# Eighty expert keys and sixty gathers ahead, a third place for weight parts between attention and the queries, and a first-block gather rate of 258/305, in a hybrid layer on Trainium2

## The chip, the cores and the metric

The kernel runs on one core of a Trainium2 chip. The metric is the device time of one execution in microseconds (us), as the median of several runs. The engines of a core run side by side, each through its own instruction list in order: TensorE (PE, with its weight loads PEld), VectorE (DVE), ScalarE (ACT), GpSimd (POOL) and SyncE (SP). They wait for each other by semaphores. DMA queues that the engines issue move the data between memory and the on-chip buffer.

## The reference, cut to what matters

One layer on x of 512 tokens by 2048, all in float32:

```python
h = hybrid_mixer(x, ...)             # mLSTM branch + forgetting attention, gated, @ w_out
x = layer_norm(DN_ALPHA * x + h, ...)
h = memory_cross_attention(x, mem, w_q, w_kv, w_o)     # 256 memory rows, 4 heads
x = layer_norm(DN_ALPHA * x + h, ...)
h = peer_ffn(x, peer_wq, sub_keys, expert_u, expert_v)
x = layer_norm(DN_ALPHA * x + h, ...)
```

The mixer's attention has 16 heads of 128 with a decay; its output Y goes through w_branch_fox and a gate. The experts (peer_ffn) are what most of the change is about. Each token has 8 heads; each picks its 16 best of 128 x 128 = 16384 experts by two lists of 128 sub-keys. With idx and g the 128 picks of a token and their weights:

```python
a = einsum('tkd,td->tk', expert_u[idx], xt)
h = gelu(a) * g
out = einsum('tk,tkd->td', h, expert_v[idx])
```

## The kernel before, in words

**Two token blocks.** Block A is the first 128 tokens, block B the other 384. A goes through the mixer, both norms, the cross attention and its expert picks early, woven into B's mixer, so that its experts' rows can be gathered while B's products run.

**Weights.** A weight comes as a raw tile of 512 KB (128 x 1024) on SP's queue (`load_raw`, L141). ScalarE rounds it to a high part `whi` (`split`, L133), VectorE subtracts to get the low part `wlo` (L134), and a product is three matmuls: high by high, high by low, low by high (`products`, L196 to L201). Other operands are split in the same way (`Ah`, `Al` by `load_split`, L136 to L139). The places for raw tiles and parts come from a list of rings, used in turn: W has 3 raw places and 2 each for `whi` and `wlo`; until the end of attention the list is W, w1 (2 raw, 1 and 1), W, and after `xs.close()` it is W alone (L1152), until the experts, when W and a ring E of the gate pool alternate.

**Pacing by weights.** `load_w` (L177 to L190) also drives gathers: for each weight loaded it adds `work["rate"]` to an account and issues as many gather steps as the account holds. The steps wait by an added dependency for the `wlo` of that weight. `residual` (L715 to L735) holds the gathers in its last two groups until the norm is done.

**Small steps.** `mid` puts small steps on a list, and `ride` takes one off for each weight loaded; a `None` is an empty turn, and `settle` runs what is left. Attention (`fox`, L580 ff) uses this. It works in quads of four heads through a written list of steps (L692): k, q, v products, S (scores, L678), g (gates of the branch), T (transposes of the probabilities and the results, L682). T(3) stands ahead of g(3), the last group. The results go to memory (`hold_r`, L1145), to `ytd`. `merge` (L700 ff) then reads `ytd` back as rows `Ah`, `Al`, five ahead (`Rows`, `load_split`), and multiplies with `w_br_fx`.

**The order.** A scheduler in the framework orders each engine's instructions by priority and simulated readiness when the kernel is compiled. On the chip each engine runs its list in that order, and a late operand holds all that is behind it.

**The experts.** A's 128 tokens are gathered in full: `gathered(0, 0, P, ...)` (L911 ff) has 258 steps: 128 rows of u (a product with the token on VectorE, L934), 128 of v (multiplied and added, L937), each row set fetched by an indirect DMA from POOL (L906), three row buffers, and a closing norm (L981 to L992) with two stores on SP's queue. It starts in the mixer of B with a rate of 258/290 steps a weight. Of B's tokens, 104 are gathered in the same way (211 steps), and 280 are taken densely: for each of the 128 keys c, `stage_a(c)` (L1279 ff) multiplies all 280 tokens with the 128 experts of that key (48 matmuls of 280 columns into `sm`), takes the gelu on ScalarE (`ga`, L1291), and for c under LOOK stores it to memory (`gad`). `stage_h` (L1297 ff) multiplies with the gates (L1308), read from `gd`, and splits the result to `hph`, `hpl`; `stage_o` takes a chunk of J = 8 keys times the v rows (`po`) and adds to `acc` (L1436).

**The gates.** The picks (`select`, with `soften`, L803 to L857, on VectorE) for B's gathered tokens come inside the query stage, those for the dense tokens after it. Then the gates are built in 70 blocks of four tokens: two comparisons on VectorE (L1253), four scalings on ScalarE (L1258), four products of 128 x 128 on PE (L1259, two records each), four copies on ScalarE (L1262), and, for each 32 tokens, stores to `gd` from ScalarE's queue (L1264). LOOK = 72 keys are done ahead of the expert chunks, and the scheduler weaves the last of them with the gates; EARLY = 56 of the 211 gather steps ride along with these keys, the rest with the chunks.

Of the kernel before, what the change touches and what calls it, by code (L numbers as in the profile page):

```python
# [10 lines left out]
F32 = mybir.dt.float32  # L11
# [10 lines left out]
P = 128  # L22
# [23 lines left out]
def build(tc, I, out):  # L46
    nc = tc.nc
    with ExitStack() as ctx:
        cp = ctx.enter_context(tc.tile_pool(name="const", bufs=1))
        dp = ctx.enter_context(tc.tile_pool(name="scratch", bufs=1, space=DRAM))  # L50
        def weights(stack, name, raw, hi, lo):

            return dict(pool=stack.enter_context(tc.tile_pool(name=name, bufs=1, reuse_waits="tile")), raw=raw, hi=hi, lo=lo)


        W = weights(ctx, "w", 3, 2, 2)
        rings = [W]
# [16 lines left out]
        def nm(s):  # L74
            cnt[0] += 1
            return f"{s}_{cnt[0]}"
# [64 lines left out]
        def load_raw(src, n=1024):  # L141
            rings.append(rings.pop(0))
            ring = rings[-1]
            raw = ring["pool"].tile([P, n], F32, tag="raw", bufs=ring["raw"], name=nm("raw"))
            nc.sync.dma_start(raw, src)
            return raw


        work = {"jobs": None, "rate": 0.0, "due": 0.0, "last": None, "hold": False,
                "quiet": 0, "normed": None}  # L150
# [12 lines left out]
        def mid(*steps):  # L163
            mids.extend(steps)
# [100 lines left out]
        for kt in range(8):  # L265
            raw = load_raw(I["xT"][kt])
# [313 lines left out]
        def fox(R, fp, ft, hold):  # L580
            n, b0, nb = R.n, R.b0, R.nb
# [71 lines left out]
            def turn_p(qd, s, kbs):  # L653
                Q = quads[qd]
                for kb in kbs:
                    f = max(kb, b0)
                    bank = sm_bank()
                    for qb in range(f, b0 + nb):
                        nc.tensor.transpose(bank[:, (qb - f) * P:(qb - f + 1) * P],
                                            Q["p"][s][qb - b0][:, kb * P:(kb + 1) * P], ident)  # L660
                    m = (b0 + nb - f) * P
                    t = fp.tile([P, m], F32, tag=f"pt{kb}", bufs=2, name=nm("fpt"))
                    if kb % 2:
                        nc.scalar.copy(t, bank[:, :m])
                    else:
                        nc.vector.tensor_copy(t, bank[:, :m])
                    Q["t"].setdefault(s, []).append(t)
# [13 lines left out]

            def T(qd):  # L682
                half = (b0 + nb + 1) // 2
                for s in range(4):
                    mid(lambda s=s: turn_p(qd, s, range(half)))
                    if s:
                        mid(lambda s=s: (result(qd, s - 1), turn_p(qd, s, range(half, b0 + nb))))
                    else:
                        mid(lambda s=s: turn_p(qd, s, range(half, b0 + nb)))
                mid(lambda: result(qd, 3))  # L690

            k, q, v, g = keys, queries, values, gates  # L692
            for step in ((k, 0), (q, 0), (v, 0), (S, 0), (g, 0), (T, 0), (k, 1), (q, 1), (v, 1), (S, 1), (g, 1),
                         (T, 1), (k, 2), (q, 2), (v, 2), (S, 2), (k, 3), (T, 2), (q, 3), (v, 3), (S, 3), (g, 2),
                         (T, 3), (g, 3)):
                work = step[0](step[1])
# [201 lines left out]
        def after(i, other):  # L898

            if other is not None:  # L900
                tc.add_manual_dep(i.ins, other.ins.name, mybir.DependencyInfo(
                    mybir.DependencyClass.Sync, mybir.DependencyReason.DATA), reason="pace")
# [8 lines left out]
        def gathered(t, r0, n, i, last, lag, keep=None):  # L911


            ei, gg = eid[:, ecols[i]], egg[:, ecols[i]]
            xacc = gat.tile([P, D], F32, tag="xacc", bufs=1, name=nm("xacc"))
            for j in range(0, P, n):
                nc.gpsimd.dma_start(xacc[j:j + n], x2d[t, r0:r0 + n].rearrange("p g c -> p (g c)"))
            dots = gat.tile([P, P], F32, tag="dots", bufs=2, name=nm("dots"))
            held = []

            def use():
                s, rows = held.pop(0)
                k = s % n
                if s == n:

                    al = gat.tile([P, 1], F32, tag="al", bufs=1, name=nm("al"))
                    if n < P:
                        nc.vector.memset(al, 0.0)
                    nc.vector.memset(al[:n], ALPHA)
                    nc.scalar.mul(xacc, xacc, al)  # L930
                    nc.scalar.activation(dots[:, :n], dots[:, :n], AF.Gelu)
                    nc.vector.tensor_mul(dots[:, :n], dots[:, :n], gg[:, :n])
                if s < n:
                    after(nc.vector.scalar_tensor_tensor(rows, rows, 1.0, xacc, op0=ALU.mult, op1=ALU.mult,  # L934
                                                         accum_out=dots[:, k:k + 1]), last())
                else:
                    after(nc.vector.scalar_tensor_tensor(xacc, rows, dots[:, k:k + 1], xacc,  # L937
                                                         op0=ALU.mult, op1=ALU.add), last())

            for s in range(2 * n):  # L940
                if len(held) == lag:
                    use()
                held.append((s, gather_rows("peer_v" if s >= n else "peer_u", ei, s % n, last)))
                yield True
            while held:
                use()
            if n < P:
                fold = gat.tile([P, 64], F32, tag="fold", bufs=1, name=nm("fold"))
                nc.vector.tensor_add(fold[:, :n], ident[:, 0:n], ident[:, n:2 * n])
                for j in range(2 * n, P, n):  # L950
                    nc.vector.tensor_add(fold[:, :n], fold[:, :n], ident[:, j:j + n])
                for g in range(4):
                    bank = BK["pool"].tile([P, 512], F32, tag="s1", bufs=1, name=nm("fo"))
                    o = xacc[:, g * 512:(g + 1) * 512]
                    nc.tensor.matmul(bank[:n], fold[:, :n], o, start=True, stop=True)  # L955
                    nc.scalar.copy(o[:n], bank[:n])  # L956
            if keep is not None:
                nc.gpsimd.dma_start(keep, xacc[:n])
                yield True
                return  # L960
            lw = fin_load(gat)
            fin_stats(i, xacc, range(4), n)
            fin(t * P + r0, i, xacc, lw, n)
            yield True
# [29 lines left out]
        def run(gen):  # L994
            for _ in gen:
                pass
# [115 lines left out]
            weave(chain(merge(A, YA, GA, ac, at), tail_a()), heads, 0.36)  # L1112

        gat = ctx.enter_context(tc.tile_pool(name="gat", bufs=1, side="right", reuse_waits="tile"))
        work.update(jobs=gathered(0, 0, P, 0, lambda: work["last"], 2), rate=258 / 290)
        run(heads)
        sgp = ctx.enter_context(ExitStack())
        sg = sgp.enter_context(tc.tile_pool(name="sg", bufs=1, side="right", reuse_waits="tile"))
# [30 lines left out]
            run(fox(B, fp, lambda n: fp.tile([P, n], F32, tag="c", bufs=16, name=nm("c")), hold_r))  # L1149
            settle()  # L1150
        xs.close()
        rings[:] = [W]  # L1152
        x3 = ctx.enter_context(ExitStack())
        apool = x3.enter_context(tc.tile_pool(name="acts_a", bufs=1, reuse_waits="tile"))
        cs = ctx.enter_context(ExitStack())
        b2 = cs.enter_context(tc.tile_pool(name="acts_c", bufs=1, side="right", reuse_waits="tile"))

# [3 lines left out]
        with tc.tile_pool(name="xb", bufs=1, reuse_waits="tile") as xp:  # L1161
# [23 lines left out]
            run(residual(B, xp, lambda t, g: x1d[t, :, g], O, zd, lambda i: a_tile(), tmp, r, sts, 4))  # L1185
            norm(B, r, sts[1], 1, x2d, cpair, tmp, X2, x2td)
        x3.close()


        NC_ = PKEYS  # L1190
# [47 lines left out]
        for hb in range(NDENSE // GB):  # L1238
            while turned * P < (hb + 1) * GB:
                bank = o_bank()  # L1240
                n = min(P, NDENSE - turned * P)
# [28 lines left out]
        acc = mn.tile([P, NK, NDENSE], F32, tag="acc", name="acc")  # L1270

        J = 8
        LOOK = 72
        EARLY = 56
        fetched, hs, gates = {}, {}, {}

        rings[:] = [W, E]
# [1 line left out]
        def stage_a(c):  # L1279
# [11 lines left out]
            nc.scalar.activation(ga, bank, AF.Gelu)  # L1291
            if c < LOOK:
                nc.scalar.dma_start(gad[c], ga)
# [3 lines left out]
        def stage_h(c):  # L1297

            for f in range(c, min(c + 3, NC_)):
                if f // 4 not in gates:  # L1300
                    gates[f // 4] = mn.tile([P, NDENSE // GB, 4, GB], F32, tag="G", bufs=2, name=nm("G"))
                    nc.sync.dma_start(gates[f // 4], gd[:, :, f:f + 4])
                if f < LOOK and f not in fetched:
                    fetched[f] = mn.tile([P, NDENSE], F32, tag="gb", bufs=4, name=nm("gb"))
# [11 lines left out]
        jobs = chain(*(gathered(TB - 1, r0, n, 1 + i, lambda: work["last"], 1, yg[r0 - FIRST:r0 - FIRST + n])  # L1316
                       for i, (r0, n) in enumerate(GATHERED)))
# [91 lines left out]
        def stage_o(c0, q, fill):  # L1409
# [3 lines left out]
            for m in range(J // 2):  # L1413
# [10 lines left out]
                products(todo, c0, c0 + J - 1)  # L1424
                if q == 3 and c0 + J < LOOK:
                    for c in (c0 + J + 2 * m, c0 + J + 2 * m + 1):
# [24 lines left out]
        njobs, done = sum(2 * n + 1 for _, n in GATHERED), 0  # L1451
        for a in range(LOOK):
            stage_a(a)
            while done * LOOK < a * EARLY:
                next(jobs, None)
                done += 1


        room = [4 if c0 < LOOK - J else 10 for c0 in range(0, NC_ - 2 * J, J) for _ in range(2 * J)]
        TOTAL, passed = sum(room), [0, 0]  # L1460
        for c0 in range(0, NC_, J):
            def fill(i, c0=c0):
# [4 lines left out]
                if room:  # L1467
                    passed[0] += room.pop(0)
                    while passed[1] < njobs - EARLY and passed[1] * TOTAL <= passed[0] * (njobs - EARLY):
                        next(jobs, None)  # L1470
# [80 lines left out]
```

## Time and profile before

| | |
|---|---|
| three runs, us | 4836.55, 4845.44, 4838.39 |
| median, us | 4838.39 |
| the profiled execution, us | 4839.64 |
| its span in the profile, us | 4837.9 |
| granted TensorE clock, mean | 0.984 |

The span goes from the first to the last instruction of one profiled execution. The engines overlap, so their shares do not add up. Idle time of an engine counts only where it holds up the end. A row of groups gives the line, engine, operation, output and inputs, count, busy time, mean of one in ns, and the idle time before with what ended it. A row of waits gives engine, tile and line, what was waited for, the sum in us, the times, and the longest. In a timeline a row begins with start and length in us. Line numbers in all rows are those of the kernel before.

### The profile page before, as it was taken

Reading aid. Unit: us, or ns where it says so; the run is one execution under the profiler, and the core shown is the slowest. Engines: PE = TensorE matmul, PEld = TensorE weight load, DVE = VectorE, ACT = ScalarE, POOL = GpSimd, SP = SyncE. Lnnn points to the kernel's source line nnn. Section 1 sums busy time; section 2 is a strip of 40 time slices with the busy share of each in tenths; the row PEclk is TensorE's granted clock in tenths of the full one; section 3 lists DMA queues with packets and bytes.
Section 4 is the critical chain, followed back from the end, with each engine's and each line's share of the span. In section 5 each row is a group of like instructions: output and inputs, shape, how many; then the busy total and the mean of one; then the engine's idle time right before and its main releaser. Section 6 shows DMA issues by size and latency. Waiting matters only on the chain. (4 is left out here: it accounts for less than half of the span.)

```text
span 4837.9 us, 75306 instructions
## 1 busy us (share of the span) xinstructions
PE 4664.7 (96%) x28717; PEld 4310.1 (89%) x28717; DVE 3763.8 (78%) x5357; ACT 2201.0 (45%) x3374; POOL 931.0 (19%) x948
## 2 busy tenths in 40 slices
PE   7999999999999899999989989999979999999998
PEld 6888888887888899999988779999969999999998
DVE  7776677666798777888769586899868998788876
ACT  6665666555543223343332334444774333433342
POOL 0000111200002332233334120221101111222220
PEclk9999999999999999999999999999989999999999
DMA  7888999865669899988889575599869999899983
GB/s 264 290 290 293 323 325 332 277 216 191 195 216 354 320 361 336 347 328 330 302 296 389 202 287 185 190 347 351 313 232 339 351 358 347 313 349 341 343 301 121
DMA packets 367663, 1432.65 MB, mean 296 GB/s; under 512 B 44255, under 2 KB 91599, under 8 KB 306803
## 3 DMA queue, kind: packets, MB, share of 16 engines
q1 hardware_dynamic: 256153, 823.27, 48.6%
q0 software_dynamic: 95008, 571.45, 31.6%
q10 hardware_dynamic: 16137, 33.10, 1.8%
q8 instruction: 225, 3.69, 0.3%
q14 instruction: 140, 1.14, 0.1%
HBM read 1343.73 MB, written 83.76 MB: 295 GB/s over the span
## 5 line engine op out<-in xcount | busy, mean ns | idle before, releaser
L133 ACT CAST whi<-raw 128x1024 fp32r<-128x1024 f32 x1472 | 1531.7, 1052 | 1831.4 <-PE mm L201 846.6
L134 DVE TENSOR_TENSOR wlo<-raw,whi 128x1024 fp32r<-128x1024 f32 x1472 | 1783.1, 1222 | 709.4 <-ACT whi L133 476.1
L937 DVE SCALAR_TENSOR_TENSOR xacc<-rows,dots,xacc 128x2048 f32<-128x2048 f32 x232 | 544.5, 2347 | 28.3 <-DMA rows<-in_peer_v,eid 27.3
L201 PE MATMUL po<-hph,whi 128*128 128x280 f32 x2048 | 533.1, 294 | 24.2 <-ACT hph L133 19.8
L934 DVE SCALAR_TENSOR_TENSOR rows<-rows,xacc 128x2048 f32<-128x2048 f32 x232 | 529.9, 2287 | 31.5 <-DMA rows<-in_peer_u,eid 31.0
L201 PE MATMUL sm<-Ch,whi 128*128 128x280 f32 x2048 | 540.4, 294 | 1.6 <-ACT xacc L956 1.3
L201 PE MATMUL sm<-Cl,whi 128*128 128x280 f32 x2048 | 539.9, 293 | 0.0
L201 PE MATMUL po<-hpl,whi 128*128 128x280 f32 x2048 | 532.0, 293 | 4.7 <-DVE hpl L134 4.7
L906 POOL DMA_INDIRECT rows<-in_peer_v,eid x232 | 351.0, 1513 | 948.6 <-DVE wlo L134 465.2
L906 POOL DMA_INDIRECT rows<-in_peer_u,eid x232 | 317.6, 1369 | 1095.1 <-DVE rows L934 542.2
L201 PE MATMUL mm<-xh,whi 128*128 128x384 f32 x1280 | 438.0, 344 | 7.6 <-ACT whi L133 4.7
L201 PE MATMUL mm<-xl,whi 128*128 128x384 f32 x1280 | 431.3, 338 | 0.0
L201 PEld LDWEIGHTS po<-hph,whi 128*128 128x128 f32 x2048 | 380.8, 190 | 28.3 <-ACT hph L133 20.6
L201 PEld LDWEIGHTS sm<-Ch,whi 128*128 128x128 f32 x2048 | 385.7, 188 | 3.8 <-ACT xacc L956 3.2
L201 PEld LDWEIGHTS po<-hpl,whi 128*128 128x128 f32 x2048 | 381.6, 190 | 6.7 <-DVE hpl L134 5.6
L201 PEld LDWEIGHTS sm<-Cl,whi 128*128 128x128 f32 x2048 | 387.0, 189 | 0.0
L201 PE MATMUL po<-hph,wlo 128*128 128x280 f32 x2048 | 336.1, 293 | 3.0 <-DVE wlo L134 3.0
L201 PE MATMUL sm<-Ch,wlo 128*128 128x280 f32 x2048 | 311.9, 293 | 1.3 <-DVE wlo L134 1.3
L201 PEld LDWEIGHTS po<-hph,wlo 128*128 128x128 f32 x2048 | 290.8, 190 | 4.9 <-DVE wlo L134 3.8
L201 PEld LDWEIGHTS sm<-Ch,wlo 128*128 128x128 f32 x2048 | 280.2, 189 | 2.7 <-DVE wlo L134 1.8
L201 PEld LDWEIGHTS mm<-xh,whi 128*128 128x128 f32 x1280 | 242.4, 190 | 14.3 <-ACT whi L133 5.0
L201 PE MATMUL mm<-xh,wlo 128*128 128x384 f32 x1280 | 255.1, 335 | 0.0
(446 smaller groups left out, 8561.5 us busy)
## 6 DMA issues: line engine op xcount, KB each, us to landing
raw<-in_w_in SPq DMA_DIRECT2D x512, 512.0 KB, 5.3
raw<-in_uT SPq DMA_DIRECT2D x256, 512.0 KB, 6.8
raw<-in_vq SPq DMA_DIRECT2D x256, 512.0 KB, 6.7
raw<-in_w_xkv SPq DMA_DIRECT2D x64, 512.0 KB, 4.9
raw<-in_w_br_ml SPq DMA_DIRECT2D x64, 512.0 KB, 5.6
raw<-in_w_br_fx SPq DMA_DIRECT2D x64, 512.0 KB, 4.9
raw<-in_w_out SPq DMA_DIRECT2D x64, 512.0 KB, 4.4
raw<-in_peer_wq SPq DMA_DIRECT2D x64, 512.0 KB, 3.9
```

The costliest lines, as they stand in the source:

```text
L133: nc.scalar.copy(hi, src)
L134: return nc.vector.tensor_sub(lo, src, hi.bitcast(F32))
L201: nc.tensor.matmul(o, w if stat else x, x if stat else w, start=k == first and x is xh and not part, stop=k == last and part == 1)
L906: i = nc.gpsimd.indirect_dma_start(out=rows, out_offset=None, in_=I[table], in_offset=bass.IndirectOffsetOnAxis(ap=ei[:, k:k + 1], axis=0))
L934: after(nc.vector.scalar_tensor_tensor(rows, rows, 1.0, xacc, op0=ALU.mult, op1=ALU.mult, accum_out=dots[:, k:k + 1]), last())
L937: after(nc.vector.scalar_tensor_tensor(xacc, rows, dots[:, k:k + 1], xacc, op0=ALU.mult, op1=ALU.add), last())
```

## The change

Five edits.

1. `load_raw` takes the pool and the number of raw places from `raw_of` of a ring, where it has one.
2. Attention of block B puts three empty turns ahead of the small steps of T(3).
3. The rate of block A's gathers goes from 258/290 to 258/305 steps a weight.
4. From the end of attention to the end of the second norm the list of rings is W, w3, W, where w3 has one `whi` and one `wlo` and shares W's raw places. After it the list is W alone, as before.
5. LOOK goes from 72 to 80 and EARLY from 56 to 60.

```diff
@@ load_raw
             ring = rings[-1]
-            raw = ring["pool"].tile([P, n], F32, tag="raw", bufs=ring["raw"], name=nm("raw"))
+            pool, bufs = ring.get("raw_of", (ring["pool"], ring["raw"]))
+            raw = pool.tile([P, n], F32, tag="raw", bufs=bufs, name=nm("raw"))
             nc.sync.dma_start(raw, src)
@@ fox, T(qd)
                 half = (b0 + nb + 1) // 2
+                if qd == 3 and b0:
+
+                    mid(None, None, None)
                 for s in range(4):
@@ ahead of run(heads)
-        work.update(jobs=gathered(0, 0, P, 0, lambda: work["last"], 2), rate=258 / 290)
+        work.update(jobs=gathered(0, 0, P, 0, lambda: work["last"], 2), rate=258 / 305)
@@ after attention of block B
         xs.close()
-        rings[:] = [W]
         x3 = ctx.enter_context(ExitStack())
         apool = x3.enter_context(tc.tile_pool(name="acts_a", bufs=1, reuse_waits="tile"))
+        rings[:] = [W, dict(weights(x3, "w3", 0, 1, 1), raw_of=(W["pool"], W["raw"])), W]
@@ after the second norm
         x3.close()
+        rings[:] = [W]
@@ experts
         J = 8
-        LOOK = 72
-        EARLY = 56
+        LOOK = 80
+        EARLY = 60
```

## Prediction, made before the changed kernel ran

> **What bounds the kernel now.** I read the page first, then its stretches as windows, then the waits of TensorE inside the stretches that the change touches.
>
> ```profile
> span 4837.9 us, 75306 instructions
> ...
> PE 4664.7 (96%) x28717; PEld 4310.1 (89%) x28717; DVE 3763.8 (78%) x5357; ACT 2201.0 (45%) x3374; POOL 931.0 (19%) x948
> ```
>
> TensorE (PE) is busy for 96% of the span. So an edit can gain only where PE idles or where it runs below its own pace, and both must be looked for by stretch. The windows from the key products to the end of the expert stage (columns: stretch, its length, busy time and count of PE, of its weight loads, of VectorE, ScalarE, GpSimd, the granted clock, DMA share, GB/s):
>
> ```profile
> core 0: us, PE busy (x) PEld busy (x) DVE busy (x) ACT busy (x) POOL busy (x), PEclk, DMA share, GB/s
> ...
> 3120.00:3405.00 285.00, 285.00 (x2221) 285.00 (x2220) 281.59 (x560) 119.06 (x151) 50.45 (x40) 1.00 0.94 348
> 3405.00:3545.00 140.00, 140.00 (x1135) 140.00 (x1134) 123.60 (x148) 113.44 (x368) 21.34 (x14) 1.00 0.85 312
> 3545.00:3609.00 64.00, 43.14 (x254) 38.51 (x253) 40.57 (x64) 55.70 (x239) 1.15 (x1) 0.89 0.39 151
> 3609.00:3624.00 15.00, 0.00 (x0) 0.00 (x0) 0.80 (x2) 0.31 (x1) 0.00 (x0) 0.55 0.86 327
> 3624.00:4041.00 417.00, 406.23 (x3075) 402.82 (x3076) 363.76 (x451) 166.15 (x215) 63.51 (x55) 0.98 0.93 344
> 4041.00:4760.00 719.00, 707.80 (x5404) 694.74 (x5402) 571.54 (x619) 281.90 (x355) 163.74 (x125) 1.00 0.89 325
> ```
>
> What to see: 3120 to 3405 is key products alone, at 285.0/2221 = 0.128 us a product, so a key of 48 products is **6.17 us**. From 3405 the gates' small products are woven into the last keys, and PE is full. From 3545 the keys have run out, and the gates stand alone: PE idles 20.9 us of 64 and the clock falls to 0.89. Then comes a stop of 15 us, then eight expert chunks with the keys already done (417/8 = **52.1 us** each) and seven in which each chunk also does its own eight keys (719/7 = **102.7 us** each). The work of such chunks at 0.128 us a product is 384 products, 49.2 us, and 768 products, 98.4 us. So a chunk loses 2.9 and 4.3 us to waits, folds and bank changes, 8 x 2.9 + 7 x 4.3 = 53 us over the stage.
>
> The second place is the junction between attention and the branch product (two windows of the same columns; 2435.6 is the last attention product of the old order, 2493.4 where PE runs full again), and what PE waited for in it:
>
> ```profile
> 2435.60:2493.40 57.80, 44.93 (x212) 39.72 (x211) 30.53 (x30) 17.05 (x31) 16.05 (x18) 0.91 0.77 271
> 2493.40:2560.00 66.60, 65.33 (x377) 64.94 (x376) 58.72 (x52) 20.68 (x24) 28.70 (x30) 1.00 0.94 359
> 2560.00:2660.00 100.00, 98.80 (x478) 86.00 (x477) 91.36 (x76) 28.60 (x32) 47.19 (x41) 1.00 0.98 385
> ```
> ```profile
> PE mm L201 <- ACT Ah L138: 8.7, 5, 3.4
> PE mm L201 <- DVE Al L139: 3.9, 4, 1.1
> PE sm L674 <- ACT y L1145: 0.2, 1, 0.2
> ```
>
> The products of the branch alone (a window of the same stretch with that tile's instructions only), and the attention results left in it:
>
> ```profile
> 2435.60:2493.40 57.80, 40.69 (x193) 0.91 0.77 271
> ```
> ```profile
> L674 PE MATMUL sm<-fpt,c 128*128 128x384 f32 (+2 forms) x16 | 4.3, 413 | 0.2 <-ACT y L1145 0.2
> ```
>
> A product of 384 columns runs at 66.6/377 = 0.177 us once it runs full. The junction holds 193 of them (34.2 us) and 4.3 us of attention's results, 38.5 us of work in 57.8: **19.3 us** are lost, 12.8 of them as idle time by the three waits, the rest at a clock of 0.91.
>
> **The change part by part.** All terms are set against the profiled execution, 4839.64 us (span 4837.9); it lies 1.2 us over the median of the three runs, 4838.39, and I take that off at the end.
>
> *Eight more keys ahead of the gates (LOOK 80).* The key products within the gates, and the gates' costliest groups, first in 3405 to 3545, then in 3545 to 3609 (columns: busy, mean ns, idle before and what ended it):
>
> ```profile
> 3405.00:3545.00 140.00, 124.45 (x806) 108.36 (x805) 0.00 (x0) 7.27 (x17) 1.00 0.85 312
> ```
> ```profile
> L1258 ACT ACTIVATE o<-o,gT 128x128 f32<-128x128 f32 x156 | 50.2, 412 | 1.2 <-DVE o L1253 0.6 <-DVE wlo L134 0.4
> L1259 PE MATMUL po<-o,o 128*128 128x128 f32 x326 | 49.4, 274 | 0.0
> ```
> ```profile
> L1259 PE MATMUL po<-o,o 128*128 128x128 f32 x235 | 41.4, 329 | 19.9 <-ACT o L1258 14.4 <-ACT stage L1262 4.8 <-DVE o L1253 0.5
> L1258 ACT ACTIVATE o<-o,gT 128x128 f32<-128x128 f32 x116 | 39.8, 493 | 4.5 <-issue 4.1 <-DVE o L1253 0.3
> ```
>
> A block of four tokens leaves eight records on line 1259. In the woven stretch 806 key products take 806 x 0.128 = 103.4 us of the 140, which leaves 36.6 us for 326 records, 0.112 us each: **0.90 us a block on PE**. In the lonely stretch 235 records are 29.4 blocks, **2.18 us a block**, paced by ScalarE (four scalings, four copies). That is what the 30 last blocks cost now.
>
> The compiled order of TensorE gives the other half. Before, 54.9 keys are done when the first gate product is issued, and 72 at block 40 of 70; after, 55.4 at the first, 72.0 at block 40, 75.6 at block 50, 79.1 at block 60 and 80 at the end. So eight keys go into the last 30 blocks. Before: 204 us (3405 to 3609), and the eight keys cost the difference of a late chunk and an early one afterwards, 102.7 - 52.1 = 50.6 us; together 254.6. After, from the same point: half a key more, 3.1; 23.7 keys and 60 blocks, 23.7 x 6.17 + 60 x 0.90 = 200.2; the last 10 blocks at ScalarE's pace, 21.8 (the last key hides in them). Together 225.1. Can the other engines follow? ScalarE was busy 113 of 140 us with 16.8 keys to 40 blocks; the next 20 blocks have 7.1 keys, nearly the same mix. I allow 3 us for their short waits. The gates' result now leaves beside more weight loads, and the 15 us stop ahead of the expert stage, which is its landing and the first multiplications, may grow; I allow the wait to stay and no more. Its row:
>
> ```profile
> PE po L201 <- ACT hph L133: 16.2, 1, 16.2
> ```
>
> Sum: 254.6 - 228.1 = 26.5 gained, **-27**; between -18 (each of the 20 newly woven blocks waits 0.4 us) and -36 (the last blocks covered too, no slack needed).
>
> *EARLY 60, and one early chunk more.* Four gather steps leave the expert stage (155 to 151). Yet they are now spread over 9 chunks of 16 weight loads and 6 of 32, and by the compiled order the rate rises from 0.42 to 0.44 rows per weight load early and 1.05 to 1.10 late, 4%. The bytes: before 417 x 0.344 + 719 x 0.325 = 377 MB. Eight keys (16 loads of 0.524 MB) and four steps of 1.05 MB leave it, with some key results through memory, about 11.5 MB; 365.6 MB in 1085 us is 337 GB/s against 332 before. That is under the 344 that the early chunks hold, but nearer to it. **+4**, from 0 to +17 (the stage shrinks only as its bytes do: 11.5/0.345 = 33 us in place of 50.6).
>
> *The third place and the delay of T(3).* What held the junction is on SP's queue (its waits from 2424 to 2494, then its issues in time):
>
> ```profile
> SPq L145 <- DVE wlo L134: 58.2, 9, 9.6
> ```
> ```profile
> 2425.67 6.78 SPq L145 DMA_DIRECT2D raw<-in_w_br_fx  x2
> 2432.54 5.35 SPq L137 DMA_DIRECT2D Al<-ytd  x5
> 2446.87 0.33 SPq L145 DMA_DIRECT2D raw<-in_w_br_fx  x1
> 2447.30 0.85 SPq L137 DMA_DIRECT2D Al<-ytd  x2
> 2451.21 0.33 SPq L145 DMA_DIRECT2D raw<-in_w_br_fx  x1
> 2451.64 0.42 SPq L137 DMA_DIRECT2D Al<-ytd  x1
> ```
>
> The weight at 2446.87 waits 9 us until an earlier one is split, and that split needs a place for its parts, of which W has two, freed by the very products that wait. The rows of Y stand behind that weight in SP's queue: a circle, one or two rows per turn. After the change the compiled order of SP has five weights, six rows, a weight, four rows, a weight, three rows; the third place lets one more weight be split ahead, and it lies in memory that attention's last stores free. Besides, 18 transposes and 3 result products of T(3) now stand behind the last group of attention (8.9 us of PE work against 4.6), so that PE has work while the first rows land. Of the 19.3 us I keep 5, for one or two stalls of 1 to 3 us at the second weight: **-14**, from -5 (the third place itself comes late) to -19.
>
> The Trainium skill speaks against a part of this: by "TensorE: Matmul & The Clock Gate", "Part 1: The HAM clock gate", half clock follows an idle window of about 3.4 us, so that waits of 3.4 us at most would leave the clock alone. By that rule the 12.8 us of waits are all there is to win, the term is -8 and the median comes to 4807, not 4801. The measured clock of 0.91 in these 57.8 us, beside 1.00 in the next two windows, says that short waits do lower it here, and I stay with the measurement.
>
> *The third place in norms and cross attention.* TensorE's waits from 2494 to 2960 for weight parts:
>
> ```profile
> PE mm L201 <- DVE wlo L134: 3.6, 4, 2.2
> ```
>
> At most this goes: **-2**, from -4 to 0.
>
> *The rate 258/305 of the first block's gathers.* Fewer steps per weight load, so they end later: the compiled order of VectorE ends them with weight 946 in place of 920, in the query stage, and between the second norm and the gates stand 51 uses in place of 40 and the closing norm of block 0. VectorE in 2925 to 3405, and the closing norm as it stands now, 2800 to 2880:
>
> ```profile
> 2925.00:3062.00 137.00, 136.59 (x814) 136.18 (x812) 80.36 (x214) 46.76 (x58) 2.19 (x5) 1.00 0.50 163
> ```
> ```profile
> L937 DVE SCALAR_TENSOR_TENSOR xacc<-rows,dots,xacc 128x2048 f32<-128x2048 f32 x13 | 30.5, 2343 | 1.1 <-DMA rows<-in_peer_v,eid 1.0
> ...
> L991 DVE SCALAR_TENSOR_TENSOR xacc<-xacc,fst,lw 128x1024 f32<-128x1024 f32 x2 | 2.5, 1282 | 0.0
> L981 DVE BATCH_NORM_STATS2 fst<-xacc 128x6 f32<-128x512 f32 x4 | 2.5, 680 | 0.0
> L990 DVE SCALAR_TENSOR_TENSOR xacc<-xacc,fst,lw 128x1024 f32<-128x1024 f32 x2 | 2.5, 1278 | 0.0
> ```
>
> Added: 11 x 2.34 + 7.5 and small steps, some 35 us on VectorE; it idles 137.0 - 80.4 = 56.6 us in the query stage, where PE is full on work that lies ahead. So it fits. Its two stores stand among the query weights in SP's queue, behind the norm: **+2**, from 0 to +8. In the first part (from the rate's start to the junction) a gather less per 19 weight loads and a slight reorder of PE: **0**, from -5 to +5.
>
> Sum: -27 + 4 - 14 - 2 + 2 + 0 = **-37**. 4839.6 - 37 = 4802.6 on the profiled execution, **4801** as a median.
>
> **The rivals.**
>
> *B, bytes pace the expert stage.* It gains 33 us, not 50.6: 17 less, against the 4 that I took, so 4801 + 13 = **4814**, and 4820 if the gates' products lose a few us to the same cause. For it: 0.93 DMA share in the early chunks. Against it: 385 GB/s in the window from 2560.
>
> *C, PE is full through gates and junction.* All terms at their good ends: -36 + 0 - 19 - 4 + 0 = -59, **about 4783** with a few us kept. For it: 140.00 of 140 us in the woven stretch.
>
> *D, the change does not do what it says.* VectorE comes late to the first gates by its added 35 us; PE takes its instructions in order, so it stands before the first gate product with the later keys behind it. 4801 + 35 = **4836**, no difference. The last of VectorE's picks ahead of the gates:
>
> ```profile
> 3392.44 0.69 DVE L844 TENSOR_REDUCE sel_i<-eq 128x32 f32<-128x512 f32 x1
> ```
>
> For it: VectorE is busy 281.6 of 285 us just ahead of the gates, and the picks end at 3393.1, only 12 us before the gates' products at 3405. Against it: the 56.6 us of idle time ahead of that.
>
> *E, slower.* The gather stream runs 4% denser through all 15 chunks; a late chunk then moves 34.9 MB (33.4 now, and 1.4 rows of 1.05 MB), which at its present 325 GB/s takes 107.4 us, not 102.7. It gets slower than before once the loss per chunk grows by (37 + 4)/15 = 2.7 us on average. If the losses of 2.9 and 4.3 us double, the stage pays 9 x 2.9 + 6 x 4.3 = 52: 4801 - 4 + 52 = **4849**. For it: the late chunks lose more each than the early ones already. Against it: 385 GB/s in a full window, and 147 us in which VectorE idles in the 719.
>
> **How the numbers follow.** Forecast, 4790 to 4810 about 4801: 0.50. B, 4810 to 4828: 0.20. C, 4780 to 4790: 0.12. D: 0.08. E: 0.10. The range of **4780 to 4828** holds the first three, 0.82. A measurement of this kernel can tell about 0.2% (9.7 us) from no change: faster means under 4828.7, which the first three are: 0.82. Same is D: 0.08. Slower, E: 0.10.
>
> **What would show it.** The lonely stretch of gates shrinks from 64 us to some 22, with eight keys between blocks 40 and 60; nine chunks of some 52 to 53 us, then six of 103 to 104 (B: 54 and 104.5 or more; E: 55 and 107); the stop behind the gates stays near 15 us; the junction takes some 43 us with a clock near 1; the query stage's PE stays full and the first gate product does not wait (D: a wait for VectorE's picks there). A stop behind the gates that grows, or a first gate product that comes 30 us late, would prove me wrong.

## The result, and the profile after

| | before | changed |
|---|---|---|
| median of 12 runs, us | 4838.77 | 4827.97 |
| lowest to highest, us | 4834.54 to 4850.82 | 4813.85 to 4832.84 |
| ratio, 95% interval | | 0.9972, 0.9962 to 0.9981 |
| the profiled execution, us | 4839.64 | 4813.85 |

The change gains 10.8 us of the 37 that were forecast. The profiled execution of the changed kernel is the shortest of its twelve, 14 us under their median. So it was run again (e1 below: 4820.32 us, ratio 0.9961, 0.9948 to 0.9973, profiled execution 4820.67), and both of its traces are used.

From here on, rows of the changed kernel and of kernels made from it carry that kernel's own line numbers: its L202, L941, L959 and L1441 are L201, L937, L955 and L1436 of the kernel before.

The page of the changed kernel, its span and its engines:

```profile
span 4812.1 us, 75372 instructions
...
PE 4656.2 (97%) x28717; PEld 4303.1 (89%) x28717; DVE 3763.1 (78%) x5357; ACT 2202.4 (46%) x3375; POOL 989.6 (21%) x948
```

Its windows from the first gate product on (columns as before):

```profile
3386.00:3510.00 124.00, 120.89 (x977) 120.47 (x976) 102.77 (x125) 95.95 (x309) 20.81 (x12) 1.00 0.83 299
3510.00:3580.00 70.00, 70.00 (x572) 70.00 (x571) 62.33 (x78) 59.57 (x204) 8.84 (x6) 1.00 0.86 302
3580.00:3613.00 33.00, 27.95 (x204) 26.71 (x202) 25.14 (x33) 30.11 (x114) 2.10 (x2) 0.95 0.71 266
3613.00:3629.00 16.00, 0.00 (x0) 0.00 (x0) 0.96 (x3) 1.06 (x6) 0.00 (x0) 0.54 0.81 312
3629.00:4099.00 470.00, 457.24 (x3458) 452.15 (x3459) 414.39 (x503) 184.54 (x238) 89.06 (x64) 0.99 0.94 350
4099.00:4734.00 635.00, 616.23 (x4633) 599.85 (x4632) 492.43 (x540) 243.53 (x307) 143.28 (x111) 0.98 0.86 316
```

What to see: the gates now have keys beside them almost to the end, and the stop of 16 us behind them has stayed. Nine early chunks take 470/9 = 52.2 us. The six late ones take 635/6 = 105.8 us where 103 to 104 were expected, and the granted clock there is 0.98, not 1.00. The starts of the chunks on TensorE's timeline say where: the six take 103.6, 98.8, 99.9, 100.7, **127.7** and 104.4 us. The seven late chunks of the kernel before take 98.7, 104.2, 98.8, 99.9, 100.7, 108.7 and 107.7 us, so it is the 14th chunk that has grown. In the window of the 14th chunk TensorE waited for this (columns: sum in us, times, longest):

```profile
PE fo L959 <- DVE xacc L941: 8.1, 1, 8.1
PE po L202 <- DVE acc L1441: 3.0, 1, 3.0
PE po L202 <- DVE wlo L134: 2.8, 1, 2.8
PE fo L959 <- ACT xacc L960: 2.0, 3, 0.7
```

The fold of a gathered group (`fo`, a small product that sums the parts of a group) waits 8.1 us for VectorE's last use of that group. TensorE's timeline there, then VectorE's (start, length, and in brackets the idle time before and what ended it):

```profile
4540.98 1.19 PE L202 MATMUL po<-hph,wlo 128*128 128x280 f32 x8
4550.32 1.92 PE L959 MATMUL fo<-xacc,fold 128*32 128x512 f32 x2 [8.14 <-DVE xacc L941]
4552.90 1.92 PE L959 MATMUL fo<-xacc,fold 128*32 128x512 f32 x2 [0.66 <-ACT xacc L960]
4555.48 1.92 PE L959 MATMUL fo<-xacc,fold 128*32 128x512 f32 x2 [0.66 <-ACT xacc L960]
4558.06 1.92 PE L959 MATMUL fo<-xacc,fold 128*32 128x512 f32 x2 [0.66 <-ACT xacc L960]
```
```profile
4537.22 2.34 DVE L941 SCALAR_TENSOR_TENSOR xacc<-rows,dots,xacc 128x2048 f32<-128x2048 f32 x1
4541.83 0.80 DVE L1441 TENSOR_TENSOR acc<-acc,po 128x280 f32<-128x280 f32 x2 [2.27 <-PE po L202]
4542.55 1.22 DVE L134 TENSOR_TENSOR wlo<-raw,whi 128x1024 fp32r<-128x1024 f32 x1
4543.69 0.79 DVE L1441 TENSOR_TENSOR acc<-acc,po 128x280 f32<-128x280 f32 x2
4544.40 1.22 DVE L134 TENSOR_TENSOR wlo<-raw,whi 128x1024 fp32r<-128x1024 f32 x1
4545.53 4.73 DVE L941 SCALAR_TENSOR_TENSOR xacc<-rows,dots,xacc 128x2048 f32<-128x2048 f32 x2
```

The same place of the kernel before, VectorE and then the first fold on TensorE, which does not wait:

```profile
4578.32 2.34 DVE L937 SCALAR_TENSOR_TENSOR xacc<-rows,dots,xacc 128x2048 f32<-128x2048 f32 x1
4580.58 1.22 DVE L134 TENSOR_TENSOR wlo<-raw,whi 128x1024 fp32r<-128x1024 f32 x1
4582.93 1.51 DVE L1436 TENSOR_TENSOR acc<-acc,po 128x280 f32<-128x280 f32 x4 [1.13 <-PE po L201]
```
```profile
4583.20 1.05 PE L955 MATMUL fo<-xacc,fold 128*32 128x512 f32 x2
```

In the changed kernel VectorE stands idle for 2.27 us ahead of the chunk's sums (`acc`), which need the products that TensorE has just issued; then come the four sums and two splits, and only then the group's last two uses. TensorE has the folds next in its list and issues nothing else until they have run. Late rows do not explain this: the group's last rows were asked for at 4533.68 us, transfers of that kind landed after 9.6 us there (median), so at about 4543, and the two uses begin at 4545.53 without idle time ahead of them. It is the compiled order of two lists: the folds stand at the same place of TensorE's list in both kernels, while on VectorE the last uses have slid from ahead of the sums to behind them.

```
VectorE before: ... use, split, split, use, split, sum, sum, sum, sum, split, (next group)
VectorE after:  ... use, sum, sum, split, sum, sum, split, use, use, (next group)
```

Windows of the same place, first of the kernel before, then of the changed kernel (columns: stretch, length, TensorE's busy time and count, granted clock, DMA share, GB/s):

```profile
4543.00:4583.00 40.00, 37.23 (x290) 1.00 1.00 394
4583.00:4591.00 8.00, 5.34 (x18) 1.00 0.68 264
4591.00:4652.00 61.00, 61.00 (x477) 1.00 0.87 268
```
```profile
4502.00:4542.00 40.00, 37.23 (x290) 1.00 1.01 394
4542.00:4564.00 22.00, 11.20 (x24) 0.59 0.58 206
4564.00:4630.00 66.00, 63.00 (x471) 0.95 0.90 288
```

The 40 us ahead of the fold are alike, at the same 394 GB/s. Then 8 us of folds have become 22, at a clock of 0.59, and the rest of the chunk takes 5 us more. 3.0 of these 5 are a second stop, the wait for `acc` in the rows above: it comes at 4601.6 us, some 40 us behind the folds.

**By stages.** The lengths below run from the first instruction of one group on TensorE's timeline to that of the next, in us, one profiled execution each.

| kernel | to the last H product | to the end of the branch | to the query | query | keys and gates | chunks and end |
|---|---|---|---|---|---|---|
| before | 1823.3 | 773.2 | 321.9 | 143.6 | 562.2 | 1213.8 |
| changed | 1812.6 | 760.0 | 318.8 | 148.2 | 589.4 | 1183.1 |
| changed again (e1) | 1815.6 | 761.6 | 316.6 | 147.7 | 590.4 | 1186.8 |
| keys alone (e2) | 1828.9 | 774.7 | 320.8 | 143.9 | 590.4 | 1188.0 |
| third place and turns alone (e3) | 1819.8 | 768.7 | 320.5 | 144.0 | 562.8 | 1213.5 |
| rate alone (e4) | 1818.8 | 766.8 | 323.6 | 148.4 | 562.9 | 1212.1 |
| EARLY 64 (e5) | 1820.7 | 759.5 | 317.8 | 147.6 | 591.0 | 1168.3 |
| LOOK 88, EARLY 72 (e8) | 1815.4 | 759.7 | 318.8 | 148.2 | 627.4 | 1110.8 |

The keys cost 27 to 28 us ahead of the chunks and give back 26 to 31: next to nothing. The two traces of the changed kernel are 25.8 and 19.0 us shorter than that of the kernel before, where the median of twelve is only 10.8 lower; no trace shows where the other executions spend the rest.

### The profile page after: what moved, and what is told of

It reads as the page before. It is cut to its first block, busy times and chain, and to the rows that moved or that the text cites. A ratio compares the mean times of both kernels' runs of the same rounds, so it can differ in the third digit from the quotient of the medians.

```text
span 4812.1 us, 75372 instructions
## 1 busy us (share of the span) xinstructions
PE 4656.2 (97%) x28717; PEld 4303.1 (89%) x28717; DVE 3763.1 (78%) x5357; ACT 2202.4 (46%) x3375; POOL 989.6 (21%) x948
## 5 line engine op out<-in xcount | busy, mean ns | idle before, releaser
L941 DVE SCALAR_TENSOR_TENSOR xacc<-rows,dots,xacc 128x2048 f32<-128x2048 f32 x232 | 544.1, 2345 | 45.3 <-DMA rows<-in_peer_v,eid 43.7
L910 POOL DMA_INDIRECT rows<-in_peer_v,eid x232 | 381.1, 1642 | 931.2 <-DVE wlo L134 519.2
L910 POOL DMA_INDIRECT rows<-in_peer_u,eid x232 | 345.7, 1490 | 1063.2 <-DVE rows L938 463.9
L202 PE MATMUL po<-hph,whi 128*128 128x280 f32 x2048 | 535.0, 294 | 28.2 <-ACT hph L133 23.5
L202 PE MATMUL sm<-Ch,whi 128*128 128x280 f32 x2048 | 544.6, 295 | 1.7 <-ACT xacc L960 1.3
L202 PE MATMUL sm<-Cl,whi 128*128 128x280 f32 x2048 | 542.9, 294 | 0.0
L202 PE MATMUL po<-hpl,whi 128*128 128x280 f32 x2048 | 533.3, 293 | 1.4 <-DVE hpl L134 1.3
L202 PE MATMUL mm<-xh,whi 128*128 128x384 f32 x1280 | 435.5, 342 | 5.9 <-ACT whi L133 3.2
L202 PE MATMUL mm<-xl,whi 128*128 128x384 f32 x1280 | 429.4, 337 | 0.0
L202 PEld LDWEIGHTS po<-hph,whi 128*128 128x128 f32 x2048 | 381.1, 190 | 31.9 <-ACT hph L133 25.2
L202 PEld LDWEIGHTS sm<-Ch,whi 128*128 128x128 f32 x2048 | 386.5, 189 | 6.6 <-ACT xacc L960 4.0
L202 PEld LDWEIGHTS sm<-Cl,whi 128*128 128x128 f32 x2048 | 387.7, 189 | 1.7 <-issue 1.7
L202 PEld LDWEIGHTS po<-hpl,whi 128*128 128x128 f32 x2048 | 381.4, 190 | 3.6 <-DVE hpl L134 2.5
L202 PE MATMUL po<-hph,wlo 128*128 128x280 f32 x2048 | 341.6, 293 | 6.6 <-DVE wlo L134 6.6
L202 PE MATMUL sm<-Ch,wlo 128*128 128x280 f32 x2048 | 315.2, 294 | 0.0
L202 PEld LDWEIGHTS po<-hph,wlo 128*128 128x128 f32 x2048 | 292.6, 189 | 9.5 <-DVE wlo L134 8.4
L202 PEld LDWEIGHTS sm<-Ch,wlo 128*128 128x128 f32 x2048 | 281.8, 189 | 0.3 <-DVE wlo L134 0.2
L202 PE MATMUL mm<-xh,wlo 128*128 128x384 f32 x1280 | 254.7, 335 | 0.0
L202 PEld LDWEIGHTS mm<-xh,whi 128*128 128x128 f32 x1280 | 241.7, 189 | 12.4 <-issue 4.3
```

Of the source, the lines that this page charges most:

```text
L202: nc.tensor.matmul(o, w if stat else x, x if stat else w, start=k == first and x is xh and not part, stop=k == last and part == 1)
L910: i = nc.gpsimd.indirect_dma_start(out=rows, out_offset=None, in_=I[table], in_offset=bass.IndirectOffsetOnAxis(ap=ei[:, k:k + 1], axis=0))
```

## The experiments

**Theory A**: the loss is the wait at the second group's fold, set by the compiled order. **Rival B**: the bytes pace the expert stage, and all chunks are longer.

**e1, the changed kernel again.** No edit.

> The changed kernel once more, for a second trace beside its own of 4813.9 us, which is 14 us under its median of 4828. Theory A (the loss of the expert stage is a static one: TensorE stands at the fold of the second gathered group in the 14th chunk, because VectorE's last two uses of that group are compiled behind the sums of that chunk): the 14th chunk again takes 120 us or more where its neighbours take 99 to 105, and the rest of the difference to the median is spread or lies in another single stop. Rival B (the bytes of the transfers pace the expert stage): every one of the six late chunks is longer by 2 us or more than the 100.7 us mean of the undisturbed ones, none by 20. About 4828 us in both.

4820.32 us, 0.9961 (0.9948 to 0.9973). The 14th chunk took 127.8 us, the four late ones ahead of it 103.6, 98.8, 99.9 and 100.7 again. That is A. Set against the kernel before in the same set of runs, the gain is 20.1 us here and 10.8 above. This trace is 6.8 us longer than the first, and that lies in no single stop: it is 3.0 us later at the end of the H products, and its chunks are 3.7 us longer. What sets the median of the twelve 14 us above the first trace, neither trace shows.

**e2, the keys alone.**

```diff
-        LOOK = 72
-        EARLY = 56
+        LOOK = 80
+        EARLY = 60
```

> Only 80 keys and 60 gathers; rings, empty turns and rate as before. Theory A: the compiled order around the second group's fold is the one of the changed kernel, so the 14th chunk takes 120 us or more here too; the gates cost 24 us more ahead of the chunks, the chunks and the tail give back 25 to 31, and the time is 4825 to 4840. Rival B: the chunks are longer one and all, 4830 to 4845, without a single long one. My forecast on record gave this part 23 us by itself, 4815.

4836.19 us, 0.9992 (0.9982 to 1.0001): no difference that can be told. The 14th chunk took 125.1 us and the fold waited 8.1 us. The early chunks were 53.0 us in the mean, 1 us longer than before. The profiled execution is the slowest of the ten, 4848.44 us. So A holds for the long chunk, and a little of B can't be excluded.

**e3, the third place and the empty turns alone** (edits 1, 2 and 4 of the change).

> Only the third place and the empty turns; keys, gathers and rate as before. The traces of before and changed say that the junction and the norms gain about 14 us between them: 4822 to 4827. If the gain ahead of the experts came from the rate instead, no difference to 4838.

4834.95 us, 0.9992 (0.9982 to 1.0002): less than expected. From the H products to the end of the branch it is 4.5 us shorter than before, not 12 to 13. In the junction TensorE waited for this:

```profile
PE mm L202 <- ACT whi L133: 5.3, 1, 5.3
PE mm L202 <- ACT Ah L138: 5.0, 2, 4.3
PE mm L202 <- DVE Al L139: 1.8, 2, 1.1
PE mm L202 <- DVE wlo L134: 1.4, 1, 1.4
```

13.5 us in all, as much as before (12.8). The waits for rows have become shorter, and a weight that is not yet split has taken their place. The changed kernel has such a wait too, of 5.6 us, but only 1.5 us for rows.

**e4, the rate alone.**

```diff
-        work.update(jobs=gathered(0, 0, P, 0, lambda: work["last"], 2), rate=258 / 290)
+        work.update(jobs=gathered(0, 0, P, 0, lambda: work["last"], 2), rate=258 / 305)
```

> Only the rate 258/305. My forecast gave 0, with 5 either way, and 2 us lost in the query stage: 4838 to 4845. If the 10 us that the changed kernel is ahead by the end of the branch product with H come from the rate, 4828 to 4834, or that much ahead there with 6 us given back in the query stage.

4833.96 us, 0.9988 (0.9978 to 0.9997). The rate, forecast at nothing, is worth as much as the third place: 6.4 us less from the H products to the end of the branch, and 4.8 us given back in the query stage. Its junction has these waits:

```profile
PE mm L201 <- ACT Ah L138: 5.5, 5, 2.2
PE mm L201 <- DVE Al L139: 5.3, 4, 2.1
```

**e5 and e6, EARLY 64 and 62 in the changed kernel.** At 64 both of VectorE's last uses stand ahead of the sums again, at 62 one of them; TensorE's list has the fold at the same place.

```diff
-        EARLY = 60
+        EARLY = 64
```

> The changed kernel with EARLY 64 in place of 60 and nothing else. In its compiled order VectorE's last two uses of the second gathered group stand ahead of the four sums of the 14th chunk's second quarter, where at 60 they stand behind them. Theory A: TensorE's wait of 8.1 us at that fold and the half clock behind it go, the 14th chunk takes some 108 us in place of 127.7, and the time falls by 16 to 20 us against the changed kernel, to about 4803. Rival B (bytes): four steps of 1.05 MB less in the chunks are worth at most 12 us at 345 GB/s and go off all chunks alike; the 14th still takes over 120.

> The changed kernel with EARLY 62. One of the two uses stands ahead of the sums, the last still behind them: from the sums' start that is four sums, one split and one use, about 5 us. Theory A: a wait of some 5 us at the second fold, a lower clock behind it, the 14th chunk 118 to 124 us, about 4814 to 4820 in all. Rival B: half way between 60 and 64 in every chunk.

EARLY 64: 4809.56 us, 0.9936 (0.9923 to 0.9950), 7 us above what I expected. The 14th chunk takes 110.3 us and the fold no longer waits for VectorE; in that chunk TensorE waited for these alone:

```profile
PE po L202 <- DVE wlo L134: 2.8, 1, 2.8
PE fo L959 <- ACT xacc L960: 2.0, 3, 0.7
PE sm L202 <- ACT xacc L960: 0.7, 1, 0.7
```

EARLY 62: 4808.98 us, 0.9929 (0.9916 to 0.9943), lower than I expected, and in the runs not apart from 64. Its trace has the half dose, as expected: the 14th chunk takes 120.3 us, with this wait:

```profile
PE fo L959 <- DVE xacc L941: 4.6, 1, 4.6
PE po L202 <- DVE wlo L134: 2.3, 1, 2.3
```

So waits of 0, 4.6 and 8.1 us go with chunks of 110.3, 120.3 and 127.7 us, about 2.2 us lost for each us of wait. The factor is not fixed: the wait of 8.1 us goes with 125.1 us in e2, where the second stop, for `acc`, is 1.7 us in place of 3.0, and with 123.4 in e12 below, which has no second stop in that chunk. Meanwhile the late chunks ahead of it are 98.8 to 103.7 us in all five traces. That decides against B. The profiled executions keep the order (span 4804.9 at 64, 4813.2 at 62); why the medians don't is open.

**e7, the changed kernel without the keys** (LOOK 72, EARLY 56).

> The changed kernel with LOOK 72 and EARLY 56 as before: the third place, the empty turns and the rate, without the keys. If the parts add up (4 and 6 us off in their runs alone), about 4828 to 4831, and the keys as they stand are worth some 5 us or nothing. If the parts help each other at the junction, as the two traces of the changed kernel suggest (12 and 13 us less from the end of the H products' last to the end of the branch products), 4824 to 4828.

4824.67 us, 0.9966 (0.9952 to 0.9979). Third place, turns and rate together are 759.9 us from the H products to the end of the branch, 13.3 less than before, where the places with the turns are 4.5 less alone and the rate 6.4. The nine traces that have all three lie between 759.4 and 761.6 us there, the two without any at 773.2 and 774.7, so this gain is clear of the scatter. And it is as fast as the whole change: the keys at EARLY 60 add nothing.

**e8, LOOK 88 and EARLY 72**, with the uses ahead of the sums.

> The changed kernel with LOOK 88 and EARLY 72, where the uses of the second group again stand ahead of the sums. Theory A with the gates filled: the last ten blocks of gates, 22 us at ScalarE's pace, take the place of some 3 keys of 6.17 us; a further chunk goes from 101 to 52 us against eight keys of 6.17 us added ahead; so 8 to 15 us below EARLY 64, if the chunks' gathers do not thicken. Rival B: the early chunks lengthen to 54 us or more and eat it: no better than EARLY 64.

4785.67 us, 0.9892 (0.9877 to 0.9907): **faster than both kernels**, and 24 us under EARLY 64 where I expected 8 to 15. Two windows of its gates, with the last blocks no longer alone:

```profile
3510.00:3580.00 70.00, 70.00 (x569) 70.00 (x568) 60.55 (x76) 57.98 (x187) 9.76 (x7) 1.00 0.83 304
3580.00:3639.00 59.00, 58.00 (x470) 57.77 (x468) 49.90 (x54) 47.03 (x154) 8.48 (x6) 1.00 0.86 313
```

Eight more keys cost 627.4 - 591.0 = 36 us ahead (49 by themselves, the rest filled idle time), and the chunks give back 57.5. Of these, 48 are one late chunk turned early, and 5.6 are the 14th and 15th chunk (106.0 and 106.2 against 110.3 and 107.5).

**e9, the changed kernel without the second group's fold.** It leaves out the fold's products and copies, and the small sums that make its matrix, so 32 tokens are not summed over their four parts.

```diff
-            if n < P:
+            if n < P and n != 32:
                 fold = gat.tile([P, 64], F32, tag="fold", bufs=1, name=nm("fold"))
```

> The changed kernel without the fold of the second gathered group: its four pairs of products on TensorE and the copies on ScalarE are left out, so the rows of 32 tokens are not summed over the four parts of a partition; the gathers and VectorE's uses stay, 60 early. Theory A: with nothing on TensorE that waits for the last use, the 14th chunk loses the 8.1 us, the 6.9 us of the folds themselves and the half clock behind, and takes 101 to 104 us, so some 24 us less than the changed kernel: about 4796 to 4800. Rival B: only the folds' own 7 us go, the 14th chunk stays near 120.

4816.58 us, 0.9951 (0.9936 to 0.9966), 17 to 21 us above what I expected of A. The 14th chunk did fall to 100.4 us, but the 15th rose to 124.8, from about 105. Its waits:

```profile
PE fo L959 <- DVE xacc L941: 15.3, 1, 15.3
PE fo L959 <- ACT xacc L960: 2.7, 3, 1.3
```

The wait moved to the next group's fold: with the second fold gone the third was compiled at another place, later on TensorE's list, and its last uses came later still. VectorE at the end of that wait:

```profile
4664.90 2.35 DVE L941 SCALAR_TENSOR_TENSOR xacc<-rows,dots,xacc 128x2048 f32<-128x2048 f32 x1 [1.71 <-DMA rows<-in_peer_v,eid]
4669.13 2.35 DVE L941 SCALAR_TENSOR_TENSOR xacc<-rows,dots,xacc 128x2048 f32<-128x2048 f32 x1 [1.88 <-DMA rows<-in_peer_v,eid]
4672.25 2.35 DVE L941 SCALAR_TENSOR_TENSOR xacc<-rows,dots,xacc 128x2048 f32<-128x2048 f32 x1 [0.76 <-DMA rows<-in_peer_v,eid]
```

Here no sum stands between the uses, and each of them waited for its rows. So e9 shows that the long 14th chunk hangs on its fold, and that a fold stops TensorE wherever it stands ahead of its last uses. It does not show the order alone at work: in this second stop rows that landed late had a part.

**e10 and e11, LOOK 96 with EARLY 80 and LOOK 104 with EARLY 84.**

> LOOK 96 and EARLY 80, the uses of the second group again ahead of the sums. Going from 80 with 64 early to 88 with 72 early took 24 us off. If what is saved is what TensorE loses while gates stand alone, that is used up at 88 (the gates end with keys still left there), and 96 only turns late chunks into early ones: a late chunk's 100.5 us against an early one's 52 and 49.4 of keys ahead is nothing, within 5 us of 4786. If late chunks themselves cost more than their keys, another 5 to 12 us.

> LOOK 104 and EARLY 84. As with 96: within 5 us of 4786 if the gates were all, further down if each late chunk loses by itself, up if more gathers are pressed into the key stage than it has bytes left for (348 GB/s there in the kernel before).

4790.05 us, 0.9897 (0.9882 to 0.9912), and 4793.85 us, 0.9901 (0.9886 to 0.9917). Both are no better than 88: 96 is within the 5 us of 4786 that I expected, 104 lies 8 above, and the reason is another. With LOOK 96 the stop behind the gates is gone as well: the wait of 15.0 us for `hph`, which LOOK 88 still has, does not appear. So the eight keys cost 34.6 us ahead of the chunks (662.0 - 627.4), not 49. The chunks, though, give back only 28.2 (1110.8 - 1082.6): the eleven early ones lie between 49.5 and 58.5 us and take 53.8 in the mean, where the ten of LOOK 88 take 52.2, and TensorE's waits in them are many short ones, the longest 6.0 us for a `wlo`. With 104 eight keys more cost 53.1 us ahead and the chunks give back 50.7; the early ones lie between 49.4 and 59.9 us, 53.7 in the mean. Why the early chunks lengthen is not shown.

**e12, the changed kernel without the empty turns** (edit 2 left out).

> The changed kernel without the three empty turns ahead of T(3). If the third place alone frees the junction, no difference to the changed kernel (0.996 to 0.997 of the kernel before). If the gain of 12 us around the junction needs the transposes and results behind the last group, the time rises by 5 to 10 us, and the branch's first rows wait as before.

4827.10 us, 0.9969 (0.9957 to 0.9981), no rise, and 767.1 us from the H products to the end of the branch, 5.5 to 7.1 more than the changed kernel's two. So third place and rate without the turns do no more there than the rate alone (766.8). The whole-time intervals of the two overlap.

## Why the prediction was wrong, point by point

The direction was right and the time lies at the edge of the range, but the forecast of -37 us was more than three times the 10.8 measured. The step that failed is the one headed "EARLY 60, and one early chunk more", +4, from 0 to +17: the two traces have +20 and +24 in its place, most of it one stop of TensorE that the term did not have. The term of the third place, -14, held only together with the rate, which was forecast at 0; without the rate it is 4.5 us.

- **Gates**: nearly right. They were to cost 24.1 us more ahead of the chunks; keys and gates together cost 27.2 and 28.2 more. The lonely stretch shrank to the last blocks, and the stop behind the gates stayed. (A key of 48 products is 6.16 us by its row, not 6.17, which changes nothing.)
- **Chunks**: wrong. Forecast 50.6 - 4 = 46.6 us less; measured 30.7 and 27.0 less. Of the 16 to 20 us that are missing, 17.4 are the 14th chunk (127.7 against 110.3 once the wait is taken away). With EARLY 64, where the fold does not wait, the chunks are 1213.8 - 1168.3 = 45.5 us shorter than before, close to the forecast, and the kernel gains 30.8 us in all. I had priced the 4% denser gathers by bytes and spread them. The bytes were not it: the undisturbed late chunks take 98.8 to 103.7 us as before. What I left out was the fold, which hangs on the last gather of a group, and where the changed EARLY would put it. The compiled order has it: VectorE's last uses of the second group behind the sums of that quarter, and TensorE's folds ahead of anything else.
- **Junction**: the size was nearly right, but in part by luck, as the reason was only half of it. Forecast 14 less; measured 13.2 and 11.6 less from the H products to the end of the branch. But the third place with the turns gives 4.5 alone, the rate 6.4 alone, and the third place with the rate but without the turns 6.1. Without the rate, or without the turns, about half of the 13 is gone; the rate and the turns without the third place were not run. How the slower rate acts is open. Fewer gathers beside the first rows and weights of the branch would be a reason, but the traces do not bear it out: between 2420 and 2500 us GpSimd issues 10 of them in the kernel before and with the rate alone, and 12 in the changed kernel.
- **Norms and cross attention**: forecast -2; 3.1 and 5.3 less. The kernel of e7, with the same third place, takes 322.1 us there, as much as before, so this is within the scatter.
- **Query**: forecast +2; 4.1 and 4.6 more. All eleven traces with the rate have 4.0 us more or above, e12 as much as 9.3; the two without it, e2 and e3, have 0.3 and 0.4. In the changed kernel most of it is a single wait, which the kernel before has not got there:

```profile
PE mm L202 <- DVE wlo L134: 3.6, 1, 3.6
```

- **The first part**: forecast 0, within 5; 10.7 and 7.7 less. The kernels with the order of before up to the H products differ there by 9 us among themselves (1819.8 and 1828.9), and the eleven with the rate by 10 (1812.6 to 1822.5), so this can't be told from the scatter of single executions.
- **The Trainium skill's rule on the clock** ("TensorE: Matmul & The Clock Gate", "Part 1: The HAM clock gate": half clock after an idle window of about 3.4 us) would have made the junction -8. The two traces have 13.2 and 11.6, but part of that came with the rate, so it is not decided here. The granted clock of 0.59 around the fold's wait of 8.1 us agrees with the rule.
- **The rivals**: The time of 4828 lies at the upper end of what B forecast, 4810 to 4828, but B did not happen: the early chunks stay at 52.2 and 52.5 us and the late ones keep their length. C did not. D did not: the gates' first product waits for no pick. E was wrong as a spread loss, but it was the right place: the gathers in the late chunks. It also held a slip: a step of a late chunk loads two weights, so the 4% are 0.7 rows a chunk, not 1.4. And in the kernel the steps are handed out over 14 chunks, 9 early and 5 late, not over all 15.

## What to carry to other kernels

Where each engine runs a fixed list, a change of counts moves every small step that hangs on the last of a series, and a few us of lateness there can cost more than their length: 13 to 17 us for 8.1 here. So compare the two lists around each such step (what stands on the producer's list ahead of the last input, and what the consumer has behind the step) before pricing the change by bytes and busy time. And when a change gains less than its parts should, look at the lengths of equal pieces one by one: five late chunks much as before and one 19 us longer (127.7 against 108.7) is a stop, not a lack of bandwidth.

## What the runs showed of the hardware

A wait of 8.1 us on TensorE cost 17.4: the clock in the 22 us around it was 0.59, the four folds came 2.58 us apart in place of 1.71, and the 48 products behind took 9.1 us in place of 6.4. That makes 8.1 + 3.5 + 2.7 = 14.3; the other 3.0 are the second stop, for `acc`, which EARLY 64 has not got. In e12, with the first stop alone, the chunk is 13.1 us longer than at EARLY 64. That the first stop caused the second is not shown. In e9 a longer wait, 15.3 us, cost about 17 to 20, so the price of a stop is not simply proportional. And in the 40 us ahead of the folds DMA moved 394 GB/s while TensorE was busy for 37.23 us; its only wait there was one of 2.8 us for a weight part.
